# Three moves of gate work in a two-layer attention kernel: gate rows, last products and gate dots

## The chip, the cores and the metric

The kernel runs on one core of one Trainium2 chip. The metric is the device time of one execution in microseconds; lower is better. The engines are called as the profile calls them: PE is the matrix engine (PEld its weight loads), DVE the vector engine, ACT the scalar engine, POOL the GpSimd engine, SP the engine whose queue issues the DMAs. `L377` is line 377 of the kernel.

## The reference

Two layers over 1024 latent tokens (and 256 context tokens) of width 1024. Each layer makes a per-channel shift, scale and gate out of a conditioning vector, projects the modulated tokens to queries, keys, values and a SiLU branch, attends with 16 heads of 64, multiplies by the branch, projects back, and adds the result to the stream under that gate, before a layer norm:

```
shift, scale, gate = jnp.split(silu_c @ w_ada[i] + b_ada[i], 3, axis=-1)
u = h * (1.0 + scale[:, None, :]) + shift[:, None, :]
...
y = (o * jax.nn.silu(g)) @ w_out
h = layer_norm(DEEPNORM_ALPHA * h + gate[:, None, :] * y, ln_g[i], ln_b[i])
```

Layer 0 attends in a window (and also updates the context tokens), layer 1 in a two-dimensional neighbourhood (and writes latent tokens only). The gate of a layer is one number per channel. The change concerns how the two gates are made and spread over the partitions.

## The kernel before, in words

Everything is in float32, and every large product is three products of high and low halves (`out_part`, L445, issues them as L451 to L453). The first layer (A) runs in 160 sub-blocks (8 pairs of heads, 10 blocks of 128 tokens, 2 heads). A sub-block `k` has three pieces: scores (`qkA`, L744), transposes of the normalised weights (`trA`, L768, which calls `sm_transpose`, L336), and the products with the values (`pvA_fn`, L775), which for each pair of sub-blocks come as a first part (from the high halves) and a second part (from the low halves, tile `ptl_A`, two buffers). `att_steps` (L803) writes them in order, `merge` (L289) weaves them with a list of other PE work, the fill, by summed cost. In the last stretch of layer A the fill ends with the output product of token block 0 (tile `yA0`), and the list of pieces ends as: transposes of 157, first part of pair 155, transposes of 158, second part of 155, transposes of 159, first and second part of 157, first and second part of 159.

Scores, transposes, gate rows and the output products of blocks 1 to 9 of layer A all take their PSUM tile from one pair of buffers (`psbig`, L97, 1024 columns each); other products use four smaller ones (`psone`).

A gate row is made by `gate_rows` (L373): eight transposes on PE of one gate column each, broadcast (L377), into a `psbig` tile, and a copy by ACT of 128x1024 to SBUF (L378). Layer A has two such rows (latent and context tokens, tile `gates`), layer B one (tile `g1`).

The gate column of layer B is made of dots: for each of 8 groups of channels and each of two halves, SP loads 128x512 of transposed weights (`gate_load`, L1229, tile `gwB`, one buffer), and one DVE instruction multiplies it with the activated conditioning and sums (`gate_dot`, L1237, the instruction at L1244; it shows as a custom DVE instruction and a read of its accumulator). They are traced from L1257, a load or a dot in every second of layer B's 128 sub-blocks of heads 0 to 8: the dots at sub-block numbers 11, 15, 19 and so on to 71, counting from where the scores are issued; a sub-block's transposes follow its scores by three.

At the end (L1334 on) eight blocks of 128 tokens are finished: POOL prepares the residual `x` (L1340, L1341, two instructions of 128x1024), PE makes the products, DVE multiplies by `g1` (L1355), adds `x` (L1356), takes statistics (L1357) and normalises (L1362, L1364), POOL takes the power for the inverse deviation (L461). Blocks 0 and 1 have most of their products done before; of them only the last group (`o7`, six products) is left.

The order of each engine's queue is not the order in the code. A planner walks a simulated time and gives each engine, whenever it is free there, the earliest traced instruction whose inputs and buffers it takes as ready. `tc.keep_in_program_order(ins)` ties an instruction behind the one traced just before it on the same engine. Once written, the queues run in order on the chip.

Of the kernel before, what the change touches and what calls it, by code (L numbers as in the profile page):

```python
# [11 lines left out]
F32 = mybir.dt.float32  # L12
# [3 lines left out]
ALU = mybir.AluOpType  # L16
# [3 lines left out]
P = 128  # L20
D = 1024
# [22 lines left out]
def f32(ap):  # L44
    return ap.bitcast(F32)
# [37 lines left out]
def build(tc, i, out):  # L83
    nc = tc.nc
# [12 lines left out]
    def psbig(name):  # L97
        return ps.tile([P, 1024], F32, tag="big", bufs=2, name=name)

    def psone(name):  # L100
        return ps.tile([P, 512], F32, tag="one", bufs=4, name=name)
# [10 lines left out]
    dcol = cp.tile([P, 32, 2], F32, name="dcol")  # L112
# [176 lines left out]
    def merge(att, fill, lead=0.0):  # L289

        ta = sum(a[0] for a in att) or 1.0
        tf = sum(f[0] for f in fill)
        ia = jf = 0
        ca = cf = 0.0
        while ia < len(att) or jf < len(fill):
            need = att[ia][2] if ia < len(att) and len(att[ia]) > 2 else 0
            if jf < len(fill) and (ia == len(att) or jf < need or cf - lead <= ca * (tf - lead) / ta):
                cf += fill[jf][0]
                fill[jf][1]()
                jf += 1  # L300
            else:
                ca += att[ia][0]
                att[ia][1]()
                ia += 1
# [65 lines left out]
    def wo_piece(wo, src, j):  # L370
        wo_split(wo, wo_load(src, j), j, (nc.gpsimd, nc.vector))

    def gate_rows(dst, src):  # L373

        pg = psbig("gate")
        for j in range(KT):
            nc.tensor.transpose(pg[:, j * P : (j + 1) * P], src[:, j : j + 1].to_broadcast([P, P]), ident)  # L377
        nc.scalar.copy(dst, pg)  # L378

    def og_load(b):  # L380
        rs = []
        for k0 in range(0, KT, 4):
            r = raw_tile("ogr").rearrange("p (k t) -> p k t", k=4)
            dma(r, ogd[k0 : k0 + 4, :, b * P : (b + 1) * P].rearrange("k p t -> p k t"))
            rs.append(r)
        return rs
# [35 lines left out]
    def og_small(rs):  # L422

        o = []
        for r in rs:
            n = r.shape[1]
            h, l = (
                wp.tile([P, 512], F32R, tag=x, bufs=4, name="og")[:, : n * P].rearrange("p (k t) -> p k t", k=n)
                for x in ("whi", "wlo")
            )  # L430
            nc.scalar.copy(h, r)
            nc.vector.tensor_tensor(l, r, f32(h), ALU.subtract)
            o += [(h[:, k], l[:, k]) for k in range(n)]
        return o
# [279 lines left out]
    def qprojA(p):  # L714
        return proj_pieces(pos["Aq", p], uA, CHUNKS, rope_evac(q_store(p), ap_, 1))

    def gprojA(p):
        def gev(pt, t0, n):
            if t0 == 0:
                gA[p] = pq.tile([P, T], F32, tag="gA", bufs=2, name=f"gA{p}")  # L720
            g_evac(ap_, gA[p])(pt, t0, n)

        return proj_pieces(pos["Ag", p], uA, CHUNKS, gev)

    def k_load(kv, l):
        k = pq.tile([P, T], F32R, tag="kA", bufs=3, name=f"kA{kv}_{l}")
        for x in range(2):
            dma(f32(k[x * 64 : x * 64 + 64]), kdA[l, kv * 64 : kv * 64 + 64, :])
        kA[kv, l] = k

    def v_loadA(kv):
        v = pq.tile([P, 10, P], F32R, tag="vA", bufs=2, name=f"vA{kv}")
        dma(f32(v), vdA[:, kv, :].rearrange("(t p) e -> p t e", p=P))
        vA[kv] = v
# [126 lines left out]
    for p in range(8):  # L861
        att = [x for row in rowsA[p * 20 : (p + 1) * 20] for x in row]
        if p % 2 == 0 and p:
            k_load(p // 2, 1)
        if p % 2 == 1 and p < 7:
            att.insert(20, (0.0, lambda p=p: k_load(p // 2 + 1, 0), 0))
            att.insert(24, (0.0, lambda p=p: v_loadA(p // 2 + 1), 0))
        if p < 7:
            n = len(att)
            for g in range(SEG[p]):  # L870
                att.insert(3 + g * (n // SEG[p] + 1), dots.pop(0))
            if not dots:
                att.append((0.0, dots_end, 0))
            merge(att, gprojA(p) + qprojA(p + 1), lead=0.0)
        else:

            att += [x for row in rowsA[8 * 20 :] for x in row]
            g7, fill = gprojA(7), []
            woA = OutWeights(up, "woA")
            for n, piece in enumerate(g7):  # L880
                fill.append(piece)
                if n >= 8:
                    fill.append((200.0, lambda j=n - 8: wo_piece(woA, i["wAo"], j)))
            assert len(fill) == G7_AT[2]
            oA0, yA0, zA0 = [], [], []

            def og_first():
                oA0.extend(og_small(og_load(0)))
                yA0.extend(psone(f"yA0_{nh}") for nh in range(2))

                for sl, x in zip(HALVES, ("whi", "wlo")):
                    zA0.append(f32(wp.tile([P, 512], F32R, tag=x, bufs=4, name="zA0")))
                    dma(zA0[-1], i["htok"][0][:, sl])

            fill.append((0.0, og_first))
            for n in range(2 * KT):
                fill.append((300.0, lambda n=n: out_part(yA0, HALVES[n // KT], oA0, woA, (n % KT,))))
            merge(att[:-6], fill, lead=1500.0)
            gts = up.tile([P, 2, D], F32, tag="l2", bufs=1, name="gates")
            for v in range(2):  # L900
                gate_rows(gts[:, v], dcol[:, 0:8, v])
            raw = og_load(1)
            merge(att[-6:], [])
    px_st.close()
# [41 lines left out]
    for b in range(10):  # L946
# [15 lines left out]
        g = gts[:, b // 8]  # L962
# [274 lines left out]
    def gate_dot(j, x):  # L1237
        t = gwB.pop((j, x))
        g, acc = gsil[:, HALVES[x]], dcol[:, 24 + j, 0:1]
        if j < 0:  # L1240
            nc.scalar.activation(t, g, AF.Tanh, scale=0.5)
            nc.vector.scalar_tensor_tensor(g, t, 1.0, g, ALU.add, ALU.mult)
            return
        nc.vector.tensor_tensor_reduce(t, t, g, 0.5, acc if x else 0.0, ALU.mult, ALU.add, accum_out=acc)  # L1244
        if j == KT - 1 and x:
            nc.vector.tensor_tensor(dcol[:, 24:32, 0], dcol[:, 24:32, 0], bad[:, 40:48], ALU.add)

# [49 lines left out]
    att = [need7(x) for x in attB[last:]]  # L1297
    fill = []
# [26 lines left out]
    ob, ob_st = pool("outB", "left")  # L1325
    vecs = []
    for j in range(4):
        t = ob.tile([P, D], F32, name=f"vec{j}")
# [5 lines left out]
    for b in range(8):  # L1334
        x = ob.tile([P, D], F32, tag="x", bufs=3, name="x")
        dma(x, grid_rows(zdd, b))  # L1336
        tok = slice(b * P, (b + 1) * P)
        if b < 6:
            parts_of[b + 2] = ogs_load(b + 2, og_home(ob, "og", 3))
        nc.gpsimd.tensor_tensor(x, x, vecs[0], ALU.mult)  # L1340
        nc.gpsimd.tensor_tensor(x, x, vecs[1], ALU.add)  # L1341
        y = [y0, y1][b] if b < 2 else [psone(f"yB{b}_{nh}") for nh in range(3 if b == 7 else 2)]
        pairs = parts_of.pop(b) + [(o7[:, 0, tok], o7[:, 1, tok])]

        cuts = (0, 512, 768, 1024) if b == 7 else (0, 512, D)
        parts = [slice(*c) for c in zip(cuts, cuts[1:])]
        for sl in parts:
            out_part(y, sl, pairs, woB, range(KT) if b > 1 else (KT - 1,))
        if b == 0:
            g1 = ob.tile([P, D], F32, name="g1")  # L1350
            gate_rows(g1, dcol[:, 24:32, 0])
        z = ob.tile([P, D], F32, tag="z", bufs=3, name="z")
        st = ob.tile([P, 3, 6], F32, tag="stat", bufs=2, name="stat")
        for j, sl in enumerate(parts):
            nc.vector.tensor_tensor(z[:, sl], part_of(y, sl), g1[:, sl], ALU.mult)  # L1355
            nc.vector.tensor_tensor(z[:, sl], z[:, sl], x[:, sl], ALU.add)  # L1356
            nc.vector.bn_stats(st[:, j, :], z[:, sl])  # L1357
        mv, rs = ln_stats(ob, st[:, : len(parts)])
        cuts = (0, 512, 1024) if b == 7 else (0, D)
        parts = [slice(*c) for c in zip(cuts, cuts[1:])]  # L1360
        for sl in parts:
            nc.vector.scalar_tensor_tensor(z[:, sl], z[:, sl], mv[:, 0:1], vecs[2][:, sl], ALU.subtract, ALU.mult)  # L1362
        for sl in parts:
            nc.vector.scalar_tensor_tensor(z[:, sl], z[:, sl], rs[:, 1:2], vecs[3][:, sl], ALU.mult, ALU.add)  # L1364
            dma(grid_rows(out, b)[:, :, sl], z[:, sl])
# [97 lines left out]
```

## Time and profile before

| | |
|---|---|
| runs | 1423.17, 1423.81, 1426.17 us, median 1423.81 |
| profiled execution | 1422.99 us |
| its span (first to last instruction) | 1421.2 us |
| PE busy | 1385.3 us, 97% of the span |
| DVE, ACT, POOL busy | 69%, 51%, 44% |
| mean granted clock of PE | 0.997 |

The profile comes from one execution, which took 1422.99 us; its span leaves out 1.8 us around it. A busy PE is modelled from pipelined products, so its idle time is best read as the gaps that the trace gives with a releaser. In the timeline a row is start, duration, engine, line, operation, tile written and tiles read, and in brackets the idle time of the engine just before and what ended it.

### The profile page before, as it was taken

How to read it: one execution, taken by the hardware profiler on the slowest of the kernel's cores; microseconds unless marked ns; L12 is line 12 of the kernel's file. 1: busy time of each engine (PE TensorE's matmuls, PEld its weight loads, DVE VectorE, ACT ScalarE, POOL GpSimd, SP SyncE). 2: the span in 40 equal slices, each digit the busy share in tenths (PEclk: the TensorE clock that was granted, in tenths of full speed). 3: DMA queues.
4: the chain of work that ended last, by engine and by line, in shares of the span. 5: the costliest groups of instructions: out<-in, count | busy, mean ns of one | idle time of the engine just before them, and what ended most of it. 6: DMA issues, size and time to landing. Idle time of an engine off the chain costs nothing. (4 is left out here: it accounts for less than half of the span.)

```text
span 1421.2 us, 25164 instructions
## 1 busy us (share of the span) xinstructions
PE 1385.3 (97%) x8816; PEld 1215.2 (86%) x8816; DVE 980.0 (69%) x2220; ACT 731.4 (51%) x1560; POOL 626.2 (44%) x776
## 2 busy tenths in 40 slices
PE   8999999999999999999999999999999999999996
PEld 6988898888988888888898899888998899888885
DVE  4658887878888789566433766566665564659598
ACT  4337776676776778432222555454454454558200
POOL 0326676667666567233211333332233232325583
PEclk9999999999999999999999999999999999999998
DMA  9572114123222114443187575564555564476753
GB/s 377 181 224 85 54 57 126 53 79 92 79 73 64 57 60 146 127 135 133 62 260 218 156 214 165 143 189 137 179 150 172 150 185 146 137 209 185 181 149 107
DMA packets 128141, 202.39 MB, mean 142 GB/s; under 512 B 9744, under 2 KB 66448, under 8 KB 128016
## 3 DMA queue, kind: packets, MB, share of 16 engines
q1 hardware_dynamic: 127872, 200.78, 47.0%
q8 instruction: 70, 1.15, 0.3%
q14 instruction: 55, 0.45, 0.1%
q10 hardware_dynamic: 144, 0.01, 0.0%
HBM read 145.18 MB, written 55.57 MB: 141 GB/s over the span
## 5 line engine op out<-in xcount | busy, mean ns | idle before, releaser
L334 POOL TENSOR_SCALAR s_B<-s_B,rs_B 128x640 f32<-128x640 f32 (+1 forms) x128 | 103.2, 806 | 289.8 <-DVE rs_B L333 262.7
L212 PE MATMUL pj<-uBh,wh 128*128 128x512 f32 (+1 forms) x448 | 175.9, 393 | 0.0
L213 PE MATMUL pj<-uBl,wh 128*128 128x512 f32 (+1 forms) x448 | 170.3, 380 | 0.0
L214 PE MATMUL pj<-uBh,wl 128*128 128x512 f32 (+1 forms) x448 | 170.1, 380 | 0.0
L329 ACT ACTIVATE s_B<-s_B,m_B 128x640 f32<-128x640 f32 (+1 forms) x128 | 102.9, 804 | 126.1 <-DVE m_B L322 125.9
L329 ACT ACTIVATE s_A<-s_A,m_A 128x641 f32<-128x641 f32 (+2 forms) x160 | 119.5, 747 | 82.9 <-DVE m_A L322 60.1
L168 POOL TENSOR_TENSOR wl<-wr,wh 128x512 fp32r<-128x512 f32 x65 | 88.2, 1358 | 158.1 <-ACT wh L163 146.4
L334 POOL TENSOR_SCALAR s_A<-s_A,rs_A 128x640 f32<-128x640 f32 (+2 forms) x160 | 128.8, 805 | 65.0 <-DVE rs_A L333 58.9
L322 DVE CUSTOM_DVE_ANT_0 s_A<-S_A,msk,nsk 128x640 f32<-128x640 f32 (+2 forms) x160 | 123.5, 774 | 32.3 <-PE S_A L755 18.2
L347 DVE TENSOR_TENSOR pt_B<-T_B,pt_B 128x640 fp32r<-128x640 f32 (+1 forms) x128 | 100.9, 788 | 60.2 <-ACT pt_B L345 59.7
L212 PE MATMUL pj<-uAh,wh 128*128 128x512 f32 (+1 forms) x384 | 140.2, 365 | 0.8 <-DVE otmp L794 0.8
L213 PE MATMUL pj<-uAl,wh 128*128 128x512 f32 (+1 forms) x384 | 137.6, 358 | 0.0
L214 PE MATMUL pj<-uAh,wl 128*128 128x512 f32 (+1 forms) x384 | 137.2, 357 | 0.0
L347 DVE TENSOR_TENSOR ptl_A<-T_A,pth_A 128x640 fp32r<-128x640 f32 (+2 forms) x160 | 114.1, 713 | 16.8 <-PE pvA L783 10.5
L341 PE MATMUL T_A<-ident,s_A 128*128 128x128 f32 x672 | 100.9, 275 | 10.7 <-DVE m_A L322 5.3
L345 ACT CAST pt_B<-T_B 128x640 fp32r<-128x640 f32 (+1 forms) x128 | 84.4, 659 | 48.2 <-PE T_B L341 47.2
L341 PEld LDWEIGHTS T_A<-ident,s_A 128*128 128x128 f32 x672 | 77.3, 140 | 37.0 <-issue 10.1
L322 DVE CUSTOM_DVE_ANT_0 s_B<-S_B,bias 128x640 f32<-128x640 f32 (+1 forms) x128 | 100.2, 783 | 8.0 <-PE S_B L1092 7.0
L345 ACT CAST pth_A<-T_A 128x640 fp32r<-128x640 f32 (+2 forms) x160 | 96.3, 602 | 17.2 <-PE T_A L341 15.7
L214 PEld LDWEIGHTS pj<-uBh,wl 128*128 128x128 f32 x448 | 84.3, 188 | 16.6
L213 PEld LDWEIGHTS pj<-uBl,wh 128*128 128x128 f32 x448 | 84.7, 189 | 9.1
L341 PE MATMUL T_B<-ident,s_B 128*128 128x128 f32 x608 | 88.1, 274 | 4.2 <-DVE pt_B L347 2.3
(224 smaller groups left out, 3866.8 us busy)
## 6 DMA issues: line engine op xcount, KB each, us to landing
kB<-kdB SPq DMA_DIRECT2D x64, 320.0 KB, 5.4
gw<-in_wadaT SPq DMA_DIRECT2D x48, 256.0 KB, 2.8
vdB<-st SPq DMA_DIRECT2D x20, 512.0 KB, 3.6
vB<-vdB SPq DMA_DIRECT2D x16, 640.0 KB, 4.6
wada<-in_wadaC SPq DMA_DIRECT2D x16, 512.0 KB, 9.6
kdB<-st SPq DMA_DIRECT2D x16, 512.0 KB, 2.8
qdB<-st SPq DMA_DIRECT2D x16, 512.0 KB, 3.7
qB<-qdB SPq DMA_DIRECT2D x32, 256.0 KB, 4.8
```

Of the source, the lines that this page charges most:

```text
L168: e.tensor_tensor(lo, r, f32(hi), ALU.subtract)
L212: mm(pt[:, :n], hi[:, sl], rh, start=kt == 0, stop=False)
L213: mm(pt[:, :n], hi[:, sl], rl, start=False, stop=False)
L214: mm(pt[:, :n], lo[:, sl], rh, start=False, stop=kt == KT - 1)
L322: nc.vector.tensor_tensor_reduce(outp, sc, in1, scale, init if init is not None else 3e38, ALU.add, ALU.min, accum_out=s.m)
L329: nc.scalar.activation(s.t[:, :n], s.t[:, :n], AF.Exp, bias=s.m, scale=-1.0, accum_out=s.sum)
L334: nc.gpsimd.tensor_scalar(s.t[:, : s.w], s.t[:, : s.w], s.rs, 1.0, ALU.mult, ALU.mult)
L341: nc.tensor.transpose(tp[:, k * P : (k + 1) * P], s.t[:, src * P : (src + 1) * P], ident)
L345: nc.scalar.copy(pt.hi[:, :n, hl, :], tv)
L347: nc.vector.tensor_tensor(pt.lo[:, :n, hl, :], tv, f32(pt.hi[:, :n, hl, :]), ALU.subtract)
```

## The change

In layer A the first gate row is traced two pieces earlier: after the transposes of sub-block 157 in place of 158, so that it stands ahead of the first part of 155 and the transposes of 158, and the second row behind the transposes of 158, as it did. The fill is woven into the list up to the transposes of 157. In layer B each gate dot is tied behind the DVE instruction traced before it. At the end the gate row of layer B is traced ahead of the six products that complete block 0, where it stood behind them. No instruction is added or removed.

```diff
-            merge(att[:-6], fill, lead=1500.0)
+
+            merge(att[:-8], fill, lead=1500.0)
             gts = up.tile([P, 2, D], F32, tag="l2", bufs=1, name="gates")
-            for v in range(2):
-                gate_rows(gts[:, v], dcol[:, 0:8, v])
+            gate_rows(gts[:, 0], dcol[:, 0:8, 0])
+            merge(att[-8:-6], [])
+            gate_rows(gts[:, 1], dcol[:, 0:8, 1])
             raw = og_load(1)
             merge(att[-6:], [])
...
-        nc.vector.tensor_tensor_reduce(t, t, g, 0.5, acc if x else 0.0, ALU.mult, ALU.add, accum_out=acc)
+
+        tc.keep_in_program_order(
+            nc.vector.tensor_tensor_reduce(t, t, g, 0.5, acc if x else 0.0, ALU.mult, ALU.add, accum_out=acc)
+        )
...
+        if b == 0:
+
+            g1 = ob.tile([P, D], F32, name="g1")
+            gate_rows(g1, dcol[:, 24:32, 0])
         for sl in parts:
             out_part(y, sl, pairs, woB, range(KT) if b > 1 else (KT - 1,))
-        if b == 0:
-            g1 = ob.tile([P, D], F32, name="g1")
-            gate_rows(g1, dcol[:, 24:32, 0])
```

## Rows read from the trace of the kernel before

**Rows 1.** The page: span, and busy time of PE with its share of the span and its instructions.

```profile
span 1421.2 us, 25164 instructions
PE 1385.3 (97%) x8816; PEld 1215.2 (86%) x8816; DVE 980.0 (69%) x2220; ACT 731.4 (51%) x1560; POOL 626.2 (44%) x776
```

**Rows 2.** Busy time in two stretches of 2 us at the gate rows of layer A: stretch, length, busy time and instructions of PE, PEld, DVE, ACT and POOL, then PE's granted clock, the DMA share and GB/s.

```profile
576.00:578.00 2.00, 1.67 (x14) 1.22 (x12) 1.76 (x4) 1.61 (x4) 0.34 (x1) 1.00 0.13 30
578.00:580.00 2.00, 1.34 (x8) 1.22 (x9) 1.31 (x3) 0.88 (x2) 0.73 (x1) 1.00 0.40 123
```

**Rows 3.** Timeline of the same place, the rows of the attention and the gate rows alone. The first row is the first part of pair 155, the transposes `T_A` are those of sub-block 158, and the products from `ptl_A` the second part of 155.

```profile
572.28 0.64 PE L783 MATMUL pvA<-pth_A,vA 128*128 128x256 f32 x4
...
573.46 0.38 PE L341 MATMUL T_A<-ident,s_A 128*128 128x128 f32 x2
...
574.38 1.04 PE L377 MATMUL gate<-ident,dcol 128*128 128x128 f32 x8
...
575.17 0.72 PE L783 MATMUL pvA<-ptl_A,vA 128*128 128x256 f32 x4
...
575.45 1.01 ACT L378 COPY gates<-gate 128x1024 f32<-128x1024 f32 x1 [0.49 <-PE gate L377]
...
575.98 0.42 DVE L347 TENSOR_TENSOR ptl_A<-T_A,pth_A 128x256 fp32r<-128x256 f32 x1 [3.36 <-PE pvA L783]
...
576.47 1.09 PE L377 MATMUL gate<-ident,dcol 128*128 128x128 f32 x8
...
577.59 1.01 ACT L378 COPY gates<-gate 128x1024 f32<-128x1024 f32 x1 [0.35 <-PE gate L377]
...
578.65 0.50 PE L451 MATMUL yA<-woAh,og 128*128 128x512 f32 x1 [0.88 <-ACT gates L378]
```

**Rows 4.** The instructions of the gate dots (the view of one tile, `gwB`): duration in ns as minimum/median/maximum, first and last start in us, form; under them how long DVE sat idle before a dot, and what ended it.

```profile
L1244 DVE CUSTOM_DVE_ANT_0 gwB<-gwB,gsil x8: 670/692/694, 762.0 to 832.5; 128x512 f32<-128x512 f32 x8
L1244 DVE CUSTOM_DVE_ANT_0 gwB<-gwB,gsil,dcol x8: 732/751/1206, 765.9 to 836.1; 128x512 f32<-128x512 f32 x8
...
  DMA gwB<-in_wadaT: 16.5, 12
```

**Rows 5.** Timeline of two places in layer B where a dot stands ahead of the low half of a transposed tile (L347).

```profile
785.60 0.56 ACT L345 CAST pt_B<-T_B 128x512 fp32r<-128x512 f32 x1
...
786.88 0.69 DVE L1244 CUSTOM_DVE_ANT_0 gwB<-gwB,gsil 128x512 f32<-128x512 f32 x1 [0.99 <-DMA gwB<-in_wadaT]
...
787.49 0.69 DVE L347 TENSOR_TENSOR pt_B<-T_B,pt_B 128x512 fp32r<-128x512 f32 x1
...
788.33 0.74 PE L341 MATMUL T_B<-ident,s_B 128*128 128x128 f32 x5 [0.94 <-DVE pt_B L347]
...
789.78 0.67 ACT L345 CAST pt_B<-T_B 128x640 fp32r<-128x640 f32 x1
...
790.38 1.21 DVE L1244 CUSTOM_DVE_ANT_0 gwB<-gwB,gsil,dcol 128x512 f32<-128x512 f32 x1 [0.30 <-DMA gwB<-in_wadaT]
...
791.51 0.81 DVE L347 TENSOR_TENSOR pt_B<-T_B,pt_B 128x640 fp32r<-128x640 f32 x1
...
792.48 0.73 PE L341 MATMUL T_B<-ident,s_B 128*128 128x128 f32 x5 [0.49 <-DVE pt_B L347]
```

**Rows 6.** Three views of layer B: who PE waited for from 755 to 850 us (total, times, longest), the same from 850 to 1000 us, and the busy time of the dots alone from 780 to 840 us (two instructions to a dot).

```profile
PE T_B L341 <- DVE pt_B L347: 1.4, 2, 0.9
...
PE T_B L341 <- DVE pt_B L347: 0.2, 1, 0.2
...
780.00:840.00 60.00, 8.55 (x22) 1.00 0.58 169
```

**Rows 7.** Timeline of the gate row of layer B and the start of the last stretch. The first row is the first of the six products that complete block 0.

```profile
1338.35 0.40 PE L451 MATMUL yB<-woBh,o 128*128 128x512 f32 x1
...
1339.74 1.04 PE L377 MATMUL gate<-ident,dcol 128*128 128x128 f32 x8
1340.22 2.38 POOL L1340 TENSOR_TENSOR x<-x,vec 128x1024 f32<-128x1024 f32 x1 [2.64 <-DMA x<-zdd]
...
1340.81 1.01 ACT L378 COPY g<-gate 128x1024 f32<-128x1024 f32 x1 [9.97 <-PE gate L377]
...
1341.86 1.29 DVE L1355 TENSOR_TENSOR z<-yB,g 128x512 f32<-128x512 f32 x2 [10.04 <-ACT g L378]
...
1342.68 2.40 POOL L1341 TENSOR_TENSOR x<-x,vec 128x1024 f32<-128x1024 f32 x1
1343.07 3.16 DVE L1356 TENSOR_TENSOR z<-z,x 128x512 f32<-128x512 f32 x2
```

**Rows 8.** The last stretch further on: a POOL and a DVE instruction that begin together; the same DVE instruction of a later block, beside no POOL work; and the end, with the last product of PE, the last multiplication by the gate row, and the last DVE instructions.

```profile
1350.32 2.47 POOL L1340 TENSOR_TENSOR x<-x,vec 128x1024 f32<-128x1024 f32 x1
1350.46 3.41 DVE L1364 SCALAR_TENSOR_TENSOR z<-z,rsd,vec 128x1024 f32<-128x1024 f32 x1
...
1408.33 1.29 DVE L1364 SCALAR_TENSOR_TENSOR z<-z,rsd,vec 128x1024 f32<-128x1024 f32 x1 [0.44 <-POOL rsd L461]
...
1410.02 0.28 PE L453 MATMUL yB<-woBh,o 128*128 128x256 f32 x1
...
1412.83 0.41 DVE L1355 TENSOR_TENSOR z<-yB,g 128x256 f32<-128x256 f32 x1
...
1415.85 1.41 DVE L1364 SCALAR_TENSOR_TENSOR z<-z,rsd,vec 128x512 f32<-128x512 f32 x2
```

More of the change, by code (lines that the diff above doesn't have):

```diff
@@ L1346, in build @@
         parts = [slice(*c) for c in zip(cuts, cuts[1:])]
-        for sl in parts:
-            out_part(y, sl, pairs, woB, range(KT) if b > 1 else (KT - 1,))
         if b == 0:
@@ L1351, in build @@
             gate_rows(g1, dcol[:, 24:32, 0])
+        for sl in parts:
+            out_part(y, sl, pairs, woB, range(KT) if b > 1 else (KT - 1,))
         z = ob.tile([P, D], F32, tag="z", bufs=3, name="z")
```

## The prediction

> **What bounds the kernel now.** I read the page first: PE is busy for 1385.3 of 1421.2 us [rows 1], so the time is PE's work, which the change leaves as it is, plus the gaps in PE's stream, some 36 us of them (1421.2 - 1385.3), plus whatever runs on after PE has ended. A move can then pay in two ways only: it closes a gap of PE, or it shortens the end. Next I read PE's waits and the timeline at the three places that the change touches. Around the gate rows of layer A, PE is idle for 0.33 and 0.66 us in two neighbouring stretches [rows 2], most of it the 0.88 us for which the first product of block 1 waits for the copy of the second gate row [rows 3]. In layer B from 755 to 850 us PE waits twice, 1.4 us in all, both times for the low half of a transposed tile on DVE [rows 6]. In the last stretch PE hardly waits, but DVE is late: it could not start before the gate row was there, after 10.04 us of idling [rows 7], and the last product of PE starts at 1410.02 while DVE reaches its part only at 1412.83 [rows 8]. So the end is set by DVE, with POOL beside it.
>
> **Layer A's gate rows.** No instruction is added; 16 transposes and two copies keep their durations. What matters is who holds the two large PSUM buffers. Before, the sequence is transposes 157, 158, first row, second row, transposes 159, block 1. The two rows follow each other through one buffer in each case: in the new order 158 sits in the other buffer. From the first row's start to block 1's first product the chain is: 1.07 us until its copy starts (574.38 to 575.45), 1.01 of copy, 0.05 to the next user (578.60 to 578.65), 1.12 for the second row up to its copy (576.47 to 577.59), 1.01 of copy, 0.05 again: 4.31 us [rows 3]. Before, that stretch took 578.65 - 574.38 = 4.27 us, so it was this same chain, with the second row also behind the low half of 158, which stood back 3.36 us for products from `ptl_A` that the first row had delayed [rows 3]. New is that the transposes of 158 and the first part of 155 now lie inside the chain, beside the first copy, where they stood ahead of it. Their rows say 0.38 and 0.64 us with modelled ends that overlap what follows; I count 0.65 us for both, an estimate. The gain is 4.27 + 0.65 - 4.31 = 0.6 us. It can't be much above the 0.99 us of idle time that is there [rows 2]. On the other side, if transposes 158 come to wait for a buffer behind a row and its copy, one chain of 1.07 + 1.01 us less the 0.65 of work beside it is added, 1.4 us lost. The fill is only woven tighter over the pieces before; one DMA, the load of block 1, keeps its place in the list and is no user of these buffers. I take 0.6, since both rows' chains can be read off [rows 3]. PE's clock is 1.00 in these stretches although 16 transposes and a gap fall into them [rows 2], so I count nothing for it.
>
> **The dots.** Sixteen dots of 0.69 or 0.75 us (medians) and a read of 0.08 each run from 762.0 to 836.8 us, and DVE idles 16.5 us in front of twelve of them for their loads [rows 4]. The planner took the loads as landed; the chip had not landed them, and DVE's queue is in order, so all behind the dot stands. It cost PE time twice. At 786.88 a dot that waited 0.99 us stood ahead of the low half that had been ready since 785.60 + 0.56 = 786.16; this started at 787.49, 1.33 us late, and PE's transposes idled 0.94 us. At 790.38 the same, with the input ready at 790.45 and the start at 791.51, 1.06 us late, and 0.49 us idle on PE [rows 5]. Tied in place, the dots start at sub-block 11, that is behind transposes 8, some 8 x 4.2 us (the two transposes of rows 5 are 4.15 us apart) after the start of the attention at about 784, and go on at one in four sub-blocks, or 17 us, until about 1070 us. A load is then issued when the dot before it has released its one buffer, 17 us ahead of its use, so no dot waits for a landing. This removes 0.94 + 0.49 = 1.4 us.
>
> What is late next is a dot on its own, 0.69 + 0.08 = 0.77 us on DVE, sixteen times, in a stretch where PE waited 0.2 us in 150 us [rows 6]. From the two stalls the slack before PE notices is 1.33 - 0.94 = 0.39 and 1.06 - 0.49 = 0.57 us, so at worst every dot costs 0.77 - 0.39 = 0.38 us, 6.1 us in all. At best it costs nothing. I take nothing: of the eleven dots that ran beside the attention (22 instructions) only these two, whose DMA was late, show a wait on PE [rows 6], and the planner, which knows the dot's duration, places PE's next transposes accordingly. SP's queue also changes: the 16 loads no longer crowd into 75 us. Each still waits in SP's queue for a dot, and stores and weight loads stand behind it, but PE did not wait for weights at all in that stretch [rows 6], with loads tied to dots four times as dense, so I count nothing. The weight columns end far ahead of their use at 1339.
>
> **Layer B's gate row.** The row moves ahead of six products. They start at 1338.35, the row at 1339.74 [rows 7], so the copy comes 1.39 us earlier and would let DVE start at 1340.5 instead of 1341.86. PE's order of work changes, not its amount; the products of block 0 end about 1 us later, at about 1340.8, still before DVE needs the second half. But DVE then meets POOL. Its first additions (L1356, two instructions, 3.16 us) start at 1343.07 and end at 1346.23, while a POOL instruction runs from 1342.68 to 1345.08 [rows 7]; further on one of DVE's takes 3.41 us beside POOL's and 1.28 us beside none [rows 8]. DVE's adds are thus held until POOL's instruction ends. In the new order the two multiplications end at 1341.75, the first add is held until POOL's first instruction ends at 1340.22 + 2.38 = 1342.60 and done at about 1343.2. If POOL's second goes next, as it did at 1350.32 against DVE's 1350.46 [rows 8], the second add waits until 1345.6 and ends at 1346.1 instead of 1346.23: 0.1 us gained. If the planner puts statistics between the adds, I work out 0.65 us (statistics and the second multiplication beside POOL, then the add). If DVE keeps going, all of block 0 is done by 1345.1 instead of about 1347.4: 2.3 us. On the bad side one more such collision costs 3.41 - 1.28 = 2.1 us. I take 0.4, between the first two, as rows 8 show POOL going in between. Since DVE sets the end, what is gained here lasts until PE's end binds: DVE's lag there, 1412.83 - 1410.3, is 2.5 us [rows 8].
>
> The Trainium skill, "SBUF — State Buffer", section "Who interferes with whom", says that a vector instruction with two SBUF inputs and a GpSimd instruction that reads SBUF exclude each other for a whole instruction, by issue order. The trace agrees (3.41 against 1.28 us), and by that rule alone, with the old order of the two adds, this part would give 0.1 us in place of 0.4.
>
> **The sum.** 0.6 + 1.4 + 0.4 = 2.4 us. The profiled execution took 1422.99 us, so it would be 1420.6. The median of the runs, 1423.81, is 0.8 us above it; from there it is 1421.4 us, which I predict. That is a gain of 0.17%; about 0.2%, or 2.85 us, is what a measurement of this kernel can tell from no change.
>
> **Rivals.** (a) The end pays in full: DVE's earlier start is kept, 2.3 us, with 1.4 and 0.6: 4.3 us, 1419.5. For it: DVE is the late engine up to the end. Against: POOL's turn between the adds. 17%. (b) Only the dots pay: the rows of layer A merely pass their wait to the transposes of 158 or 159, and POOL takes back the end; 1.0 to 1.4 us, about 1422.6. For it: the chain of two rows is the same length as before. 24%. (c) Slower: the dots inside the attention each hold the low half of a transposed tile (L347) and so PE's transposes. Up to 6.1 us lost with 2.4 gained gives 1427.5; it decides from 2.4/16 = 0.15 us a dot. For it: slack of 0.39 to 0.57 us against 0.77 us. Against: nine dots beside the attention that cost nothing. 11%. (d) The change doesn't do what it says: a dot is tied only behind the DVE instruction traced before it, and if that one is early the dot stays early and still waits for its load: 1.0 us from the rest, 1422.8. 4%. The forecast has the remaining 44%, with 1419.9 to 1422.9 as its own range.
>
> **Chances and range.** Faster by over 2.85 us: nearly all of (a), 16%, a good third of the forecast, 16%, and 4% from the spread of the runs under (b) and (d): 36%. Slower by over 2.85 us: 9% from (c) and 3% from a new order that the planner hits upon: 12%. Within: 52%. The range reaches from the better part of (a) to the milder part of (c): 1418.3 to 1425.8 us.
>
> **What would show it.** Dots: no wait for `in_wadaT` on DVE, starts spread from about 815 to 1070 us, and no wait of PE at 780 to 800. If PE's waits for L347 from 815 to 1070 exceed 2 us, (c) holds. Layer A: the time from the transposes of 157 to block 1 is shorter by 0.6 us, with the first copy beside the transposes of 158. End: the copy of the row starts 1.4 us earlier relative to the six products; the gap from the last product's start to the end of DVE (1417.26 - 1410.02 = 7.2 us) shrinks by as much as this part pays. It is wrong if the time rises, or if the end shrinks by 2 us or more.

## The result and the profile after

The changed kernel takes 1429.33 us (median of five runs, 1428.24 to 1430.55) where the kernel before, run beside it, took 1423.81: a ratio of 1.0036, 95% interval 1.0024 to 1.0048. It is slower by some 5.1 us. The forecast was 1421.4. Its profiled execution took 1429.33 us, 6.3 more than that of before. In the experiments below two executions of 6976.72 and 6010.39 us, far outside all others, are left out of every figure.

The page of the changed kernel, beside [rows 1]:

```profile
span 1427.2 us, 25161 instructions
...
PE 1386.8 (97%) x8816; PEld 1215.6 (85%) x8816; DVE 980.6 (69%) x2220; ACT 730.7 (51%) x1560; POOL 627.7 (44%) x776
```

PE has 1.5 us more of modelled busy time (with the same 8816 products) in a span that is 6.0 us longer. The rest is gaps, and a later end. To find where, I lined up marks of PE in both traces (starts of given transposes). The differences of after to before in us: up to the transposes of layer A's sub-block 140, +1.87, where both kernels still run the same instructions, so this is spread from one execution to another; from there to the first `uT` transposes, which follow the output products of block 1, +2.52; to layer B's first transposes, +0.02; sub-blocks 0 to 8, -1.78; 8 to 64, +1.23; 64 to 127, -0.20; from there to the end of the span, +2.38. The sum is the 6.04 us of the spans.

**Layer A.** Two stretches of the changed kernel, from the transposes of 140 to those of 152 and on to those of 157 (columns as in rows 2):

```profile
526.23:561.73 35.50, 31.98 (x217) 28.34 (x217) 30.56 (x65) 30.62 (x64) 26.53 (x36) 1.00 0.37 124
561.73:577.79 16.06, 15.73 (x91) 13.43 (x92) 11.37 (x30) 9.65 (x23) 6.24 (x13) 1.00 0.43 131
```

The same two stretches of the kernel before:

```profile
524.36:558.21 33.85, 33.02 (x221) 29.46 (x222) 30.18 (x66) 31.00 (x64) 26.28 (x35) 1.00 0.43 137
558.21:571.37 13.16, 13.06 (x83) 11.26 (x82) 10.57 (x28) 9.19 (x23) 7.24 (x13) 1.00 0.40 129
```

In the first stretch the changed kernel has less PE work (31.98 against 33.02 us) and takes longer (35.50 against 33.85): PE is idle for 3.5 us where it was idle for 0.8. In the second it has the missing work, and more, to do. Both kernels have 98 products of the fill behind the transposes of 140. Before, 59 of them lie in the first stretch, 30 in the second and 9 between the transposes of 157 and 159; in the changed kernel it is 51, 44 and 3. So the second stretch takes 8 from the first, and 6 from behind it. Whom PE waited for in the first stretch of the changed kernel (total, times, longest):

```profile
PE T_A L341 <- DVE m_A L322: 2.0, 4, 1.0
PE T_A L341 <- POOL s_A L334: 0.7, 1, 0.7
PE pvA L783 <- ACT pth_A L345: 0.4, 1, 0.4
```

Before, PE had one such wait in both stretches together, 0.5 us for `m_A`. So the transposes come due before DVE's row maxima and POOL's scaling are done, and no fill stands ahead of them. The gate rows themselves, in the timeline of the changed kernel, beside [rows 3]:

```profile
578.71 1.04 PE L377 MATMUL gate<-ident,dcol 128*128 128x128 f32 x8
...
579.50 0.72 PE L783 MATMUL pvA<-pth_A,vA 128*128 128x256 f32 x4
...
579.79 1.01 ACT L378 COPY gates<-gate 128x1024 f32<-128x1024 f32 x1 [0.49 <-PE gate L377]
...
580.06 0.38 PE L341 MATMUL T_A<-ident,s_A 128*128 128x128 f32 x2
...
580.85 1.09 PE L377 MATMUL gate<-ident,dcol 128*128 128x128 f32 x8
...
581.98 1.01 ACT L378 COPY gates<-gate 128x1024 f32<-128x1024 f32 x1
...
583.04 0.50 PE L451 MATMUL yA<-woAh,og 128*128 128x512 f32 x1 [0.28 <-ACT gates L378]
```

From the first row to block 1's first product it is 583.04 - 578.71 = 4.33 us, and the first part of 155 (579.50) and the transposes of 158 (580.06) lie inside it.

**The dots.** The tile `gwB` and PE's waits from 815 to 1080 us in the changed kernel, beside [rows 4] and [rows 6], and one of the places where PE waited:

```profile
L1248 DVE CUSTOM_DVE_ANT_0 gwB<-gwB,gsil x8: 674/684/694, 820.6 to 1077.0; 128x512 f32<-128x512 f32 x8
L1248 DVE CUSTOM_DVE_ANT_0 gwB<-gwB,gsil,dcol x8: 734/745/1450, 838.9 to 1093.9; 128x512 f32<-128x512 f32 x8
```

```profile
PE T_B L341 <- DVE pt_B L347: 0.9, 3, 0.5
```

```profile
984.96 1.75 POOL L168 TENSOR_TENSOR wl<-wr,wh 128x512 fp32r<-128x512 f32 x1
...
985.14 0.69 ACT L345 CAST pt_B<-T_B 128x640 fp32r<-128x640 f32 x1
...
985.81 1.45 DVE L1248 CUSTOM_DVE_ANT_0 gwB<-gwB,gsil,dcol 128x512 f32<-128x512 f32 x1
...
987.19 0.81 DVE L347 TENSOR_TENSOR pt_B<-T_B,pt_B 128x640 fp32r<-128x640 f32 x1
...
988.15 0.74 PE L341 MATMUL T_B<-ident,s_B 128*128 128x128 f32 x5 [0.49 <-DVE pt_B L347]
```

The dots now start from 820.6 to 1093.9 us and none waits for its load. But PE waits three times, 0.9 us in all, where before it waited once, 0.2 us, from 815 to 1080 us. The largest of the three is behind a dot: POOL's split of weights ends at 984.96 + 1.75 = 986.71, the dot that began at 985.81 takes 1.45 us where the median is 0.745, and the low half behind it, ready at 985.83, starts at 987.19. The other two, 0.20 us each (at 950.83 and 1051.61), have no dot straight ahead of the low half.

**The end.** The timeline of the changed kernel, beside [rows 7] and [rows 8] (its L1361, L1362, L1368 and L1370 are L1355, L1356, L1362 and L1364 of before, L1345 and L1346 are POOL's L1340 and L1341):

```profile
1342.02 1.04 PE L377 MATMUL gate<-ident,dcol 128*128 128x128 f32 x8
...
1342.81 0.48 PE L451 MATMUL yB<-woBh,o 128*128 128x512 f32 x1
1343.09 1.01 ACT L378 COPY g<-gate 128x1024 f32<-128x1024 f32 x1 [8.58 <-PE gate L377]
...
1344.14 1.89 DVE L1361 TENSOR_TENSOR z<-yB,g 128x512 f32<-128x512 f32 x3 [8.65 <-ACT g L378]
...
1345.09 2.40 POOL L1345 TENSOR_TENSOR x<-x,vec 128x1024 f32<-128x1024 f32 x1 [3.83 <-DMA x<-zdd]
...
1345.94 4.89 DVE L1362 TENSOR_TENSOR z<-z,x 128x512 f32<-128x512 f32 x2
...
1347.56 2.73 POOL L1346 TENSOR_TENSOR x<-x,vec 128x1024 f32<-128x1024 f32 x1
```

and further on:

```profile
1368.33 3.33 POOL L1345 TENSOR_TENSOR x<-x,vec 128x1024 f32<-128x1024 f32 x1 [3.28 <-DMA x<-zdd]
...
1371.73 2.39 POOL L1346 TENSOR_TENSOR x<-x,vec 128x1024 f32<-128x1024 f32 x1
...
1374.09 0.55 POOL L461 TENSOR_TENSOR rsd<-rsd,half 128x1 f32<-128x1 f32 x1
...
1374.67 3.42 DVE L1370 SCALAR_TENSOR_TENSOR z<-z,rsd,vec 128x1024 f32<-128x1024 f32 x1 [4.67 <-POOL rsd L461]
```

The row does stand ahead of the products now (1342.02 against 1342.81), and DVE starts 1.4 us earlier against PE's stream. But its first two additions take 4.89 us, under both of POOL's instructions on `x`, in place of 3.16. And at 1374.67 the normalisation has waited 4.67 us for the power of block 2 (`rsd`, L461), which stands in POOL's queue behind the two `x` instructions of block 3. DVE's waits from 1336 us to the end, first in the kernel before, then in the changed one:

```profile
DVE z L1364 <- POOL rsd L461: 1.8, 4, 0.4
```

```profile
DVE z L1370 <- POOL rsd L461: 6.4, 5, 4.7
```

### The profile page after: what moved, and what is told of

Same layout as the page of the kernel before. It is cut to its first block, busy times and chain, and to the rows that moved or that the text cites. A ratio compares the mean times of both kernels' runs of the same rounds, so it can differ in the third digit from the quotient of the medians.

```text
span 1427.2 us, 25161 instructions
## 1 busy us (share of the span) xinstructions
PE 1386.8 (97%) x8816; PEld 1215.6 (85%) x8816; DVE 980.6 (69%) x2220; ACT 730.7 (51%) x1560; POOL 627.7 (44%) x776
## 4 chain that ended last, share of the span: by engine, by line
PE 76%; DVE 10%; ACT 4%; issue 4%; POOL 3%; DMA 3%; DVEq 0%; SPq 0%; ACTq 0%; POOLq 0%
PE pj L214 10%; PE pj L213 10%; PE pj L212 10%; PE T_A L341 4%; PE T_B L341 4%; PE pvB L1128 4%; PE pvA L783 3%; PE pv L250 3%; PE pv L249 3%; PE pv L248 3%; PE yA L451 2%; PE yA L452 2%; PE yA L453 2%; PE S_A L754 2%; PE S_B L1093 2%
## 5 line engine op out<-in xcount | busy, mean ns | idle before, releaser
L347 DVE TENSOR_TENSOR pt_B<-T_B,pt_B 128x640 fp32r<-128x640 f32 (+1 forms) x128 | 100.9, 789 | 59.1 <-ACT pt_B L345 58.7
L347 DVE TENSOR_TENSOR ptl_A<-T_A,pth_A 128x640 fp32r<-128x640 f32 (+2 forms) x160 | 114.2, 714 | 15.0 <-PE pvA L783 7.1
L212 PEld LDWEIGHTS pj<-uBh,wh 128*128 128x128 f32 x448 | 84.5, 189 | 9.1
```

The source lines that it names most:

```text
L212: mm(pt[:, :n], hi[:, sl], rh, start=kt == 0, stop=False)
L347: nc.vector.tensor_tensor(pt.lo[:, :n, hl, :], tv, f32(pt.hi[:, :n, hl, :]), ALU.subtract)
```

## The experiments

Each ratio is to the kernel before on the same chip, with its 95% interval; 0.1% is 1.4 us.

**One part at a time.** The first three kernels each hold one hunk of the diff above. The fourth puts the first row of layer A early, but weaves the fill as before:

```diff
-            merge(att[:-6], fill, lead=1500.0)
+            att.insert(len(att) - 8, (0.0, lambda: gate_rows(gts[:, 0], dcol[:, 0:8, 0]), 0))
+            merge(att[:-6], fill, lead=1500.0)
...
-            for v in range(2):
-                gate_rows(gts[:, v], dcol[:, 0:8, v])
+            gate_rows(gts[:, 1], dcol[:, 0:8, 1])
```

Layer A's part: 

> Only the layer A edit (fill woven up to the transposes of 157, first gate row two pieces earlier). Theory W (the new weave of the fill costs, not the rows): slower than before by 2.0 to 3.0 us, about 1426.3; between the transposes of sub-blocks 140 and 157 some 4.5 us are lost, and about 2 come back by the first product of block 1. Rival (the forecast's step, weave free): faster by 0.6 us, 1423.2. Rival (the dots carry the whole loss): no change within 1 us.

The dots: 

> Only the dots tied in place. Theory (forecast's step, with a small price per dot): faster by 0.5 to 1.4 us, about 1423.0; no wait of PE from the start of layer B's attention to its ninth transposes, and 0.5 to 1.2 us lost between sub-blocks 8 and 64. Rival (the dots carry the loss): slower by 3 to 6 us, 1427 to 1430.

The row of layer B: 

> Only layer B's gate row ahead of the six products. Theory Q (the planner now queues a load of x behind an output store on SP, and POOL's power behind POOL's work on that x): slower by 2 to 3 us, about 1426.3; DVE waits over 4 us once for the power, one load of x is issued 10 us later than before. Rival (the forecast's step): faster by 0.4 us. Rival (the tail's loss comes with the dots or layer A): no change within 0.5 us.

The early row with the old weave: 

> The first gate row of layer A at the changed kernel's place (behind the transposes of 157), but the fill woven as before, up to the transposes of 158. Theory W: not slower than before, 0 to 1 us faster, about 1423.3, with no loss between sub-blocks 140 and 157. Rival (the row's place costs, since it holds one of the two large PSUM buffers among the last transposes): slower by 1.5 to 3 us as in the layer A edit alone.

Measured: layer A 1.0022 (1.0013 to 1.0030), 3.1 us slower; the dots 0.9999 (0.9991 to 1.0008); the row of layer B 1.0020 (1.0011 to 1.0029), 2.9 us slower; the early row with the old weave 1.0004 (0.9995 to 1.0013). The three parts add to 0.41%, against 0.36% of the whole. So two parts lose, each more than the gain that the forecast had for all three. The dots alone change nothing that can be measured: the 0.5 to 1.4 us expected of them did not come in the times, though both of the trace's signs did (no wait of PE from 755 to 850 us, and a loss of some 1.1 us from sub-block 8 to 64). For the early row with the old weave the times don't tell 0 to 1 us of gain from none, but the 1.5 to 3 us of loss of its rival lie at the end of their interval (1.9 us) or beyond.

**The weave alone**, both gate rows where they stood:

```diff
-            merge(att[:-6], fill, lead=1500.0)
+            merge(att[:-8], fill, lead=1500.0)
+            merge(att[-8:-6], [])
```

> The kernel before with only the weave changed: the fill is woven into the pieces up to the transposes of 157, then the first part of 155 and the transposes of 158 follow without fill, and both gate rows stand where they stood. Theory W (the shorter list of pieces makes the loss, since all the fill is pressed between fewer pieces of attention and the transposes come to wait for DVE and POOL): 2.5 to 3.5 us slower than the kernel before, that is 1427 to 1428, with PE idle 3 us or more between the transposes of sub-blocks 140 and 157, where the kernel before has 0.9. Rival (the row between the pieces makes the loss together with the weave, by splitting the last pieces): no more than 0.8 us slower, and the whole loss only where row and weave come together.

Measured 1.0025 (1.0016 to 1.0035), 3.6 us slower. From the transposes of 140 to the first `uT` it takes 68.40 us in this run, 68.41 with layer A's whole part, 68.33 in the changed kernel, 65.80 before, and 64.91 with the early row and the old weave. So the weave makes all of layer A's loss, and the row's place by itself gained 0.9 us in the trace. The first stretch from 140 to 152 has the changed kernel's numbers:

```profile
524.16:559.65 35.49, 32.03 (x217) 28.40 (x217) 30.53 (x65) 30.69 (x64) 26.53 (x36) 1.00 0.37 124
```

and the run with the early row and the old weave those of before:

```profile
525.39:559.11 33.72, 32.96 (x220) 29.48 (x221) 30.19 (x66) 30.93 (x64) 26.30 (x35) 1.00 0.44 138
```

**The end, first theory.** In the changed kernel SP issues block 3's load of `x` at 1359.43, behind the first output store, which waits for DVE until 1358.10; in the kernel before it went out at 1346.29, ahead of the first store. I took this for the cause and put the stores on ACT's queue, with the row in its old and in its new place, and in the new place together with the dots and the early row of layer A with the old weave:

```diff
-            dma(grid_rows(out, b)[:, :, sl], z[:, sl])
+            nc.scalar.dma_start(grid_rows(out, b)[:, :, sl], z[:, sl])
```

Old place: 

> The kernel before, with the stores of the output blocks issued from ACT's queue instead of SP's, so that no load of x stands behind a store that waits for DVE. Theory Q (a load of x behind a waiting store is what makes the end late when the gate row is moved): nothing or a small gain here, 0 to 1.5 us faster, since in the kernel before the load of block 3 is issued ahead of the stores anyway; only the later loads come sooner. Rival P (POOL's order is what counts: the small power instruction of block 1 ahead of block 3's two x instructions): this kernel has the new POOL order too, so it would be 2 to 3 us slower than the kernel before.

New place: 

> The gate row of layer B ahead of the six products, as in the changed kernel, and the output stores on ACT's queue. Theory Q: the loss of 2.9 us that the row alone made is gone; the time is that of the kernel before with stores on ACT's queue, less what DVE's earlier start is worth, 0 to 1.4 us; so -2.5 to +0.3 us against the kernel before. Rival P (POOL and DVE shut each other out in a worse order when DVE begins earlier): still 2 to 3 us slower than the kernel before.

All moves: 

> The three moves with the two suspected costs taken out: the first gate row of layer A ahead of the first part of 155 with the fill woven as before, the dots held in place, the row of layer B ahead of its products, and the output stores on ACT's queue. If the weave and the store in front of the load are the whole loss, the parts add up: 0 for the row of layer A (+0.6 measured, within its interval), 0 for the dots (-0.4), and the end as in the run with the row of layer B and stores on ACT's queue: -3 to +0.5 us against the kernel before. If another interaction between the parts costs time, it is slower than the kernel before by more than 1 us.

Measured: old place 0.9990 (0.9981 to 0.9999), new place 1.0015 (1.0006 to 1.0024), all moves 1.0000 (0.9992 to 1.0009). The row still loses: the runs of the two places differ by 3.4 us in the mean (95% 2.5 to 4.4, resampled from the runs). The first theory fell. The run of all moves falls in its expected range for another reason than the one given: its end is as late as with the row alone (95.84 us from the transposes of 127 to DVE's end, against 95.99, and 92.69 with the row in its old place), and it is the dots and the early row of layer A that bring it 2.15 us below that run (1.2 to 3.1). What is left is to be seen in POOL's timeline of the run with the new place:

```profile
1363.24 2.39 POOL L1340 TENSOR_TENSOR x<-x,vec 128x1024 f32<-128x1024 f32 x1
1365.71 3.26 POOL L1341 TENSOR_TENSOR x<-x,vec 128x1024 f32<-128x1024 f32 x1
1368.95 2.85 POOL L1340 TENSOR_TENSOR x<-x,vec 128x1024 f32<-128x1024 f32 x1
1371.87 3.27 POOL L1341 TENSOR_TENSOR x<-x,vec 128x1024 f32<-128x1024 f32 x1
1375.10 0.55 POOL L461 TENSOR_TENSOR rsd<-rsd,half 128x1 f32<-128x1 f32 x1
```

and in DVE's:

```profile
1375.68 3.41 DVE L1364 SCALAR_TENSOR_TENSOR z<-z,rsd,vec 128x1024 f32<-128x1024 f32 x1 [2.20 <-POOL rsd L461]
```

With the load early, POOL takes four instructions on `x` in a row, and the power of block 2 stands behind all four; DVE waits 2.20 us for it.

**The end, second theory: POOL.** Two pairs with work left out: without POOL's instructions on `x` (the residual unscaled), and without its power:

```diff
-        nc.gpsimd.tensor_tensor(x, x, vecs[0], ALU.mult)
-        nc.gpsimd.tensor_tensor(x, x, vecs[1], ALU.add)
```

```diff
-        mv, rs = ln_stats(ob, st[:, : len(parts)])
+        mv = ob.tile([P, 2], F32, tag="mv", bufs=2, name="mv")
+        rs = ob.tile([P, 2], F32, tag="rsd", bufs=2, name="rsd")
+        nc.vector.bn_aggr(mv, st[:, : len(parts)])
+        nc.vector.tensor_scalar(rs[:, 1:2], mv[:, 1:2], EPS, None, ALU.add)
```

Without `x`, row in its old place: 

> The kernel before without POOL's two instructions on x in the last stretch: the residual goes in unscaled and without its shift, so the output is another one, and POOL has only the small power instructions there. DVE's additions then meet no POOL instruction. In the kernel before DVE is busy without a gap from 1341.9 to the end; its 34 two-input instructions (multiplications and additions, 33.0 us) would take about 23 us at 0.69 us each (0.41 for the narrow ones), the normalisations 23 instead of 29 us, so DVE is no longer late and the end is bound by PE's last product and one block's tail: 4 to 6 us faster than the kernel before.

New place: 

> The same without POOL's x instructions, with the gate row of layer B ahead of its products. Theory X (what the earlier row loses is made by POOL's x instructions: they shut DVE out, and the small power instruction stands behind them): no loss is left, within 0.6 us of the run without x and with the row in its old place. Rival Y (the loss is made on PE or in DVE's own order of instructions): 1.5 to 3 us slower than that run.

Without the power, old place: 

> The kernel before without POOL's power instruction in the last stretch: DVE writes the variance itself, so the output is another one, and DVE never waits for POOL's queue, while POOL's x instructions stay and still shut DVE out. The kernel before shows DVE waits for the power of about 0.44 us in five blocks and a POOL instruction of 0.5 to 1.5 us less in each: 1 to 4 us faster than the kernel before.

New place: 

> The same without the power, with the gate row of layer B ahead of its products. Theory X1 (the loss is the time for which DVE waits for the power behind two or four x instructions, 2.2 to 9.6 us of idle DVE in the runs with the earlier row): the loss is gone, -1.4 to +0.5 us against the run without the power and with the row in its old place. Theory X2 (the loss is that DVE's first two additions fall under both x instructions of block 2, 4.89 instead of 3.16 us, and others like it): 1.2 to 2.5 us slower than that run.

Measured: without `x` 0.9968 (0.9955 to 0.9980) and 0.9972 (0.9961 to 0.9984); without the power 0.9984 (0.9975 to 0.9992) and 0.9981 (0.9972 to 0.9990). In both pairs the loss of the earlier row is gone: +0.5 us (-0.7 to 1.7) without `x`, -0.05 (-1.1 to 1.0) without the power. So the loss needs POOL's work. The pair without `x` is the weaker evidence: DVE is no longer late there, and would hide a loss of its own. Without the power DVE is still late (it idles for 1.6 of the 74.0 us from its first multiplication to its end), and the times show no loss. DVE's groups in the last stretch (busy time, mean ns of one, idle before), in the kernel before:

```profile
L1356 DVE TENSOR_TENSOR z<-z,x 128x512 f32<-128x512 f32 x15 | 21.1, 1413 | 0.3
L1364 DVE SCALAR_TENSOR_TENSOR z<-z,rsd,vec 128x1024 f32<-128x1024 f32 x7 | 15.2, 2175 | 1.8 <-POOL rsd L461 1.8
...
L1355 DVE TENSOR_TENSOR z<-yB,g 128x512 f32<-128x512 f32 x15 | 10.1, 676 | 10.0 <-ACT g L378 10.0
```

and without `x`, row in its old place:

```profile
L1354 DVE TENSOR_TENSOR z<-z,x 128x512 f32<-128x512 f32 x15 | 10.2, 687 | 0.3
L1353 DVE TENSOR_TENSOR z<-yB,g 128x512 f32<-128x512 f32 x15 | 10.2, 685 | 23.4 <-PE yB L453 13.0 <-ACT g L378 10.0
L1362 DVE SCALAR_TENSOR_TENSOR z<-z,rsd,vec 128x1024 f32<-128x1024 f32 x7 | 9.0, 1282 | 1.8 <-POOL rsd L461 1.8
```

The additions, with both inputs in SBUF, fall from 1413 to 687 ns, the second normalisation from 2175 to 1282; the multiplications, which read PSUM, have 676 and 685. DVE then waits for PE, and an earlier row has nothing to give.

The pair without the power left one thing open: its two profiles, against the times, have the end (from sub-block 127's transposes to DVE's last) at 91.59 and 93.79 us. In the second DVE waits once, 2.3 us, for `x` of block 3 itself, whose load stands behind a store. So a late load can cost without any power, in that execution at least. The last four runs keep the whole computation and make the inverse deviation on ACT:

```diff
-        mv, rs = ln_stats(ob, st[:, : len(parts)])
...
+        nc.vector.tensor_scalar(rs[:, 0:1], mv[:, 1:2], EPS, None, ALU.add)
+        nc.scalar.activation(rs[:, 0:1], rs[:, 0:1], AF.Ln)
+        nc.scalar.activation(rs[:, 1:2], rs[:, 0:1], AF.Exp, scale=-0.5)
```

Row in its old place: 

> The kernel before with the inverse deviation of the last stretch made on ACT (logarithm, then exponential of minus half of it), which is idle there, in place of POOL's power: nothing of the layer norm stands in POOL's queue any more. Where the profile has DVE wait 0.44 us for the power in five blocks, the way over ACT may be as long or longer, but no power stands behind x. 0.5 to 2.5 us faster than the kernel before; if ACT's two instructions take longer than POOL's one and DVE has nothing to do meanwhile, up to 3 us slower.

New place: 

> The same with the gate row of layer B ahead of its products. Theory X1 (the power behind x is the loss): within 1 us of the run with the row in its old place, or up to 1.4 us faster. Theory X2 (additions shut out under x): 1.5 to 3.5 us slower than that run.

Old place, dots held, early row of layer A with the old weave: 

> The dots held, the first row of layer A ahead with the fill woven as before, the row of layer B where it was, the inverse deviation on ACT. If the parts add: the run with ACT alone, -0.4 for the dots, +0.6 to -0.8 for the row: within 1.2 us of that run. It beats the kernel before where ACT alone does.

The same with the new place: 

> All three moves, with the weave as before and the inverse deviation on ACT. X1: as fast as the run of ACT with the dots and the first row, or up to 1.4 us faster. X2: 1.5 to 3.5 us slower than that.

Measured: 1.0000 (0.9991 to 1.0009), 0.9995 (0.9986 to 1.0004), 0.9996 (0.9987 to 1.0005) and 0.9986 (0.9978 to 0.9995). The first is a miss: with the row in its old place ACT gains nothing, where 0.5 to 2.5 us were expected. With the power off POOL's queue the earlier row gains: 1.1 us in the first pair (95% from 2.3 gained to none), 1.7 in the second (0.6 to 2.8). That agrees with the 1.39 us of its earlier start. The planner writes a new order in these runs too, so they show that the loss goes with the power's place, not how many of its microseconds are waits and how many additions under `x`. No run moved the row with POOL's and SP's order held as it was, so the order and the power are not told apart further.

DVE's idle time between its first multiplication and its end says the same in the traces. It is 2.9 us in all six profiles with the power on POOL and the row in its old place, 5.2 to 12.4 us in the four with the row in its new place, and 3.3 to 3.4 us in all four with the power on ACT, wherever the row is. From the first multiplication to DVE's end it is 75.1 to 77.0, 79.2 to 81.2, and 75.3 to 77.5 us. DVE's waits in the run with the new place alone:

```profile
DVE z L1355 <- ACT g L378: 8.6, 1, 8.6
DVE z L1369 <- ACT rsd L1363: 1.6, 3, 0.6
```

The last version, with all three moves, the weave of before and the power on ACT, is the fastest with the whole computation: 1422.18 us against 1425.13 for the kernel before beside it, 2.0 us by the ratio.

## Why the prediction was wrong

**The fill.** The step that failed in layer A is "The fill is only woven tighter over the pieces before": counted as nothing, it cost 2.5 us in the trace (68.33 - 65.80) and 3.6 in the run of the weave alone. I looked at who holds the PSUM buffers and not at what covers DVE's and POOL's part of each sub-block. The fill is that cover. With the list two pieces shorter, fill went out of sub-blocks 140 to 152 into those behind, PE stood 3.5 us in the first in place of 0.8, and what the second stretch did in addition was only work moved into it. Why the planner's order sends the fill later I did not follow; that the weave and nothing else makes the loss is shown by the two runs that split it from the row.

**The chain of the two rows** was right: 4.31 us forecast, 4.33 measured, with 158 and the first part of 155 inside. Its gain of 0.6 is seen only with the old weave, as 0.9 us in the trace; the times of that run, 1.0004 with an interval of some 0.1% to each side, can't tell it from nothing. The gain repeats: from the transposes of 140 to the first `uT` it is 64.86 to 65.23 us in all four profiles with the early row and the old weave, and 65.67 to 66.17 in the eleven with neither the early row nor the new weave. With the new weave it was gone: the weave alone and the whole part take the same 68.4 us.

**The dots.** The two stalls went, as predicted: sub-blocks 0 to 8 take 32.65 us in place of 34.42, 1.8 gained where the sum had 1.4. "I take nothing" for the dots in the attention was the term too small: sub-blocks 8 to 64 take 255.06 us in the changed kernel and 255.20 with the dots alone, against 253.84 before and 253.65 to 254.52 in the other runs of one part and in that of the weave, about 1.1 us lost. PE's waits for L347 make 0.7 us of it (0.9 against 0.2), but only the largest, 0.49, is plainly rival (c)'s mechanism, and there it is not the dot's 0.77 us but a dot held by POOL. Where the rest is lost stays open. The mark of 2 us that I had set for (c) was not reached. In the times the dots alone come to 0.01%.

**Both terms together.** Three pairs of runs differ only in the held dots and the early row of layer A with the old weave: row of layer B early and stores on ACT, power on ACT, and power on ACT with the row of layer B early. With both moves the runs are 2.2, 1.0 and 1.6 us faster, 1.6 in the mean (95% 1.0 to 2.2, resampled). The two single runs, added, say 0.2 us slower (1.3 faster to 1.8 slower). So the pairs bear out most of the 2.0 us that the forecast had for these two terms, with the old weave; the single runs don't, and why they differ stays open.

**The end.** "I take 0.4" failed, and with it the claim that DVE's gain lasts until PE's end binds. The row did come 1.38 us earlier (14.09 us after the transposes of 127, before 15.47). Two things went against it. First, the additions: I built on the 3.16 us of the one profile [rows 7]; in eight other profiles with the row in its old place they take 3.93 to 4.23 us, in seven with the new place 4.17 to 5.53. POOL begins the first of its two instructions when its load has landed, 17.2 us after the transposes of 127 in the changed kernel (1345.09) and 17.2 with the early row of layer A alone (1342.68): an earlier DVE only meets more of POOL. (The 0.1 us that I worked out from that row was nothing already: a second addition that starts at 1345.6 and takes the 0.69 us of one beside no POOL work ends at 1346.3, not 1346.1.) Over the whole stretch of the changed kernel this did not cost: DVE is busy for 71.6 us from its first multiplication to its end, before 72.5, as its later normalisations ran shorter (1894 ns in the mean, before 2175).

Second, and larger, the power: I priced collisions of instructions, and not POOL's queue, in which a power on 128x1 stands behind 5.8 us of `x` (1368.33 to 1374.09), with the stores on ACT behind 11.9. The planner wrote another order after the move: block 1's power, which had stood between the two `x` instructions of block 3, now stands ahead of both, and block 3's load behind a store. DVE has little slack to take that: in the kernel before it idles for 2.9 of the 75.4 us from its first multiplication to its end, in the changed kernel for 7.6 of 79.2. My bad side, one more collision at 2.1 us, was too small: the part cost 2.9. The mark that I had named shows it: from the last product's start to DVE's end it was 7.24 us, and is 1423.33 - 1412.97 = 10.36. (The 7.24 is itself a low reading: in four other profiles whose end is not changed it is 7.95 to 8.88; with the row of layer B alone moved it is 11.60.)

```profile
1412.97 0.28 PE L453 MATMUL yB<-woBh,o 128*128 128x256 f32 x1
...
1421.92 1.41 DVE L1370 SCALAR_TENSOR_TENSOR z<-z,rsd,vec 128x512 f32<-128x512 f32 x2
```

**The rivals and the range.** No rival had this: (c) put a loss on the dots, and "a new order that the planner hits upon" had 3%. Both losses come with a new order that the planner writes after a move in the code; the range ended at 1425.8 since I priced the moves and not the reordering that they set off.

## What to carry over

Where a planner orders the queues, a move in the list changes more than what moves: before pricing it, ask which work covers the waits of the stretch that gets shorter, and which small instruction of a shared engine comes to stand behind large ones. Starting a late engine earlier pays only if what it waits for later comes earlier too; here the gate row lost 2.9 us while the power was on POOL and, in the means of two pairs, gained 1.1 and 1.7 with it on ACT. And one profile is one execution: lay several beside each other, if they can be had, before a row of a microsecond carries a step.

## What was not expected of the hardware

The same instruction stream, up to sub-block 140, came out between 0.2 us shorter and 1.9 us longer than in the profile of before, over seventeen profiles of kernels that differ only behind it.

The way over ACT costs it two table loads for each block, in the run with the new place alone:

```profile
1350.11 0.20 ACT L1362 ACTIVATE rsd<-rsd 128x1 f32<-128x1 f32 x1 [6.83 <-DVE rsd L1361]
1350.33 1.28 ACT L1363 ACT_TABLE_LOAD   x1
1351.63 0.20 ACT L1363 ACTIVATE rsd<-rsd 128x1 f32<-128x1 f32 x1
1351.85 1.28 ACT L1362 ACT_TABLE_LOAD   x1
```

That is 1.28 us twice beside 0.20 us of each function, and yet DVE waits only 1.6 us in all, since one load is made ahead of time and ACT has nothing else to do. The Trainium skill, "ScalarE: Activation LUTs", section "What ACT_TABLE_LOAD costs", has about 1.28 us for the load, which agrees; the drain of some 1.38 us that it adds does not show between these rows.

The way in which DVE and POOL hold each other up is not confined to the end: a dot of two SBUF inputs took 1.45 us, ending 0.55 after POOL's split, and PE waited 0.49 us behind it.
